# RWKV scan: larger VectorE products, copies on ScalarE, a norm's scratch in another buffer, and a 32-column operand

## The chip, the cores and the metric

One Trainium2 chip, one core. The metric is the device time of one execution in microseconds: the median of several runs. A core has TensorE (PE, matmuls), VectorE (DVE), ScalarE (ACT), GpSimd (POOL), SyncE (SP, here the queue of the DMAs), a memory SBUF of 128 partitions, and PSUM banks into which TensorE writes.

## What is computed

The reference is a network of two layers over 1024 latent tokens and 256 context tokens of width 1024. Each layer normalises, modulates with vectors made from the conditioning input (`ada_w`, `ada_b`), projects, mixes tokens with four groups side by side (mLSTM, Hyena, retention, RWKV-7), projects back, and runs a convolutional feed-forward block. What the change touches:

```
mod  = split(silu_c @ ada_w[l] + ada_b[l], 6)
u    = modulate(layer_norm(x), mod[0], mod[1])
...
sa    = einsum('bhvk,bhk->bhv', s_mem, at)
s_new = s_mem*wt[:,:,None,:] + sa[...,None]*bt[:,:,None,:] + vt[...,None]*kt[:,:,None,:]
y     = einsum('bhvk,bhk->bhv', s_new, rt)
...
out = g * (head_group_norm(from_heads(h), ng, nb) + bonus)
```

The middle part is the RWKV-7 recurrence, run forward and backward over the tokens, first over the context and then over the latent tokens, 4 heads of width 64. All is in float32.

## The kernel before

**Stages.** A layer runs: modulation vectors and layer norms; the input projections, each as three matmuls over high and low halves of both operands (lines 1022 to 1024); the scan stage (RWKV scan, mLSTM and, as side work, the modulation vectors that come later); output projection; feed-forward. In the profiled execution layer 0's scan stage lies at about 760 to 1240 us, layer 1's at 2945 to 3390 us.

**The RWKV scan** works in ten steps of 128 tokens, forward and backward direction together (index `d`), and two chunks of 64 in each step. Per step:

- `rwkv_prep` (L472): decays, the operands `ar` (tile AR) and `bk` (tile BK), and their products `G` on TensorE. `bk` is multiplied by a part of `rkk` (L515) and by a decay (L526).
- `rwkv_inverse` (L546): the inverse of a unit triangular matrix. LM is a transposed copy of `NB` (L550, VectorE); 31 rounds of a product (L557) and a sum (L558) follow, each on what the one before left, most of it on GpSimd (62 instructions), a smaller part on VectorE. LM has one buffer.
- `rwkv_tail` (L562): transposes of the inverse into XT, two groups of small matmuls with Q between them, and four copies of corners into XT, in turn on ScalarE (L590) and VectorE (L591).
- `rwkv_chain` (L594): the recurrence, four times one after the other (two chunks, two directions). Each takes U (L614), a matmul, two copies into VSA (L617, the first on ScalarE, the second on VectorE), and an update of the state SV with the factor rho (L624). rho comes from four small products per step (L601), into one of two buffers.
- `group_norm` (L645) for two tiles of 128 tokens at a time, as soon as both directions of them are summed in YF: after steps 1 (layer 0 alone), 6, 7, 8 and 9. Its scratch is `gq`, which then goes out by DMA to `yw` (L659). Scratch and LM lie in the same pool under different names.

In the program's text a step s runs inverse(s+1), chain(s), group norm, tail(s+1), prep(s+2). **The order that runs is made by a scheduler**: it estimates times and puts each engine's instructions in one order, in which they then run; waits between engines are semaphores, and a buffer that is taken again waits for those who used it before. So a small edit can move instructions of other stages.

**Modulations.** `ada_steps` (L958) takes, per unit, 16 matmuls (L973) with the 128x128 weights as the loaded operand's partner and `k.sc[:,q]`, 2 columns (token and context), as the operand that is loaded; it leaves two rows of results at partitions 0 and 32 of a bank. `ada_out` (L937) copies them to `ab` (L940, two VectorE copies of 2x128), transposes (L941), and adds the bias (L944). `ada` (L948) does the same with larger blocks at the kernel's start.

**The layers' ends.** The output weights `wo` are loaded and split into halves in 32 pieces (`load_wo`, L1037: ScalarE L1015, VectorE L1016) into memory that the mLSTM's tiles hold until it has ended.

Of the kernel before, what the change touches and what calls it, by code (L numbers as in the profile page):

```python
# [429 lines left out]
def rwkv(K,l,pv,last,p1,p2,p3):  # L430
# [39 lines left out]
def rwkv_prep(K,C,s):  # L470
# [42 lines left out]
    for a in range(2):  # L513
        for ft in range(2): act(out=bk[:,:,ft,:,a],in_=As[:,:,ft].rearrange("p d (c t) -> p d c t",t=64),func=ACTF.Identity,scale=C['kas'][:,a,0,ft:ft+1],bias=C['kas'][:,a,1,ft:ft+1])
        for d in range(2): tt(out=bk[:,d,:,:,a],in0=bk[:,d,:,:,a],in1=v4(rkk[:,d,4-2*a:6-2*a]),op=A.mult)  # L515
    G=p.tile([128,2,2,2,2,128],F32,tag="G",name="G",bufs=3); bt=p.tile([128,2,2,2,2,64],F32,tag="BKT",name="bt",bufs=3)
    NB=p.tile([128,2,4,32],F32,tag="NB",name="NB")
    for d in range(2):
# [7 lines left out]
        for a in range(2): tt(out=bk[:,d,:,:,a],in0=bk[:,d,:,:,a],in1=Wi,op=A.mult)  # L526
# [34 lines left out]
def rwkv_tail(K,C,P):  # L561
# [26 lines left out]
    for q in range(2):  # L588
        lo=slice(q*64,q*64+32); hi=slice(q*64+32,q*64+64)
        act(out=XT[lo,0,:,hi],in_=bv[lo],func=ACTF.Copy)  # L590
        nc.vector.tensor_copy(out=XT[hi,1,:,lo],in_=bv[hi])  # L591


def rwkv_chain(K,C,P,Pn,s):  # L594
# [4 lines left out]
    for i in range(2):  # L599
        if i and not Pn: break  # L600
        for d in range(2): tt(out=rho[:,i,d],in0=io[:,1,d,:,i^d],in1=(Pn if i else P)['io'][:,0,d,:,d if i else 1-d],op=A.mult)  # L601
    need_y=not(C['last'] and s<2); YF=C['YF']
    if need_y: y=K.ybank(); yb=[y[:,0:256],y[:,256:512]]
    for i in range(2):
        for d in range(2):
# [11 lines left out]
            act(out=VSA[0:64,d,ch,0],in_=bv[0:64],func=ACTF.Copy); nc.vector.tensor_copy(out=VSA[64:128,d,ch,1],in_=bv[64:128])  # L617
# [310 lines left out]

def ada_bias(k,todo,pool):

    o=load_rows(k,[((l,g),rows(k.a['ada_b'][l:l+1,g*1024:g*1024+1024]),8) for l,g in todo],"adab",pool)
    for l,g in todo:
        if g in (1,4): k.nc.vector.tensor_scalar(out=o[l,g],in0=o[l,g],scalar1=1.0,scalar2=None,op0=ALU.add)
    return o


def ada_out(k,l,c0,n,ps,ab,t,bias):  # L937

    nc=k.nc; G=ab.shape[0]//32; e=n//128
    for j in range(G): nc.vector.tensor_copy(out=ab[32*j:32*j+2],in_=ps[32*j:32*j+2,0:n])  # L940
    for i in range(e): nc.tensor.transpose(t[:,i*G*32:(i+1)*G*32],ab[:,i*128:i*128+128],k.ident[0:G*32,0:G*32])  # L941
    m,j0=c0//1024,c0%1024//128
    tv=lambda v: v.rearrange("p (j i) s -> p j i s",i=e)
    nc.vector.tensor_tensor(out=tv(k.modc[:,m,j0:j0+G*e]),in0=t[:,0:e*G*32].rearrange("p (i j r) -> p j i r",i=e,r=32)[:,:,:,0:2],  # L944
        in1=tv(bias[l,m][:,j0:j0+G*e].unsqueeze(2).to_broadcast([128,G*e,2])),op=ALU.add)


def ada(k,l,g,pool,ab,loads,bufs,bias):  # L948

    nc=k.nc; b=k.dbank()  # L950
    for q in range(8):
# [451 lines left out]
def tile_backbone(ctx,tc,aps,out):  # L1403
# [42 lines left out]
```

## Time and profile before

| | us |
|---|---|
| median of 3 runs | 4264.0 |
| lowest, highest | 4252.06, 4266.33 |
| the profiled execution | 4269.9 |
| its span (first to last instruction) | 4268.0 |
| TensorE busy | 3956.8 (93%) |
| VectorE busy | 2672.2 (63%) |
| ScalarE busy | 1416.9 (33%) |
| GpSimd busy | 979.7 (23%) |

The shares are averages over stages of different kinds: the projections keep TensorE full, the scan stages don't. In a row of a profile, L550 is line 550, `LM<-NB` says which tile is written from which, and what stands after "idle before" or in square brackets is how long the engine stood idle just before and what ended that.

### The profile page before, as it was taken

Reading aid. Unit: us, or ns where it says so; the run is one execution under the profiler, and the core shown is the slowest. Engines: PE = TensorE matmul, PEld = TensorE weight load, DVE = VectorE, ACT = ScalarE, POOL = GpSimd, SP = SyncE. Lnnn points to the kernel's source line nnn. Section 1 sums busy time; section 2 is a strip of 40 time slices with the busy share of each in tenths; the row PEclk is TensorE's granted clock in tenths of the full one; section 3 lists DMA queues with packets and bytes.
Section 4 is the critical chain, followed back from the end, with each engine's and each line's share of the span. In section 5 each row is a group of like instructions: output and inputs, shape, how many; then the busy total and the mean of one; then the engine's idle time right before and its main releaser. Section 6 shows DMA issues by size and latency. Waiting matters only on the chain.

```text
span 4268.0 us, 65334 instructions
## 1 busy us (share of the span) xinstructions
PE 3956.8 (93%) x24976; PEld 3210.9 (75%) x24976; DVE 2672.2 (63%) x5412; ACT 1416.9 (33%) x2855; POOL 979.7 (23%) x2158
## 2 busy tenths in 40 slices
PE   5999999699979999999997999996899899999998
PEld 3878877566668888888884688885666678888886
DVE  5655665789769444444449555676888684444447
ACT  4433343554344211211123433344544342112121
POOL 3320023466512000000021221024666320000002
PEclk6999999789989999999998999997899699999999
DMA  4235444343343111111113235553332431111112
GB/s 166 74 102 177 149 153 122 112 143 116 122 160 119 45 40 34 41 40 35 37 35 124 82 91 154 169 162 114 122 115 84 136 114 55 48 41 55 45 50 99
DMA packets 477138, 414.16 MB, mean 97 GB/s; under 512 B 48827, under 2 KB 443284, under 8 KB 474010
## 3 DMA queue, kind: packets, MB, share of 16 engines
q1 hardware_dynamic: 476826, 409.99, 31.0%
q8 instruction: 197, 3.23, 0.3%
q14 instruction: 115, 0.94, 0.1%
HBM read 323.65 MB, written 86.25 MB: 96 GB/s over the span
## 4 chain that ended last, share of the span: by engine, by line
PE 52%; DVE 11%; DMA 3%; issue 2%; POOL 1%; ACT 1%; SPq 0%; ACTq 0%; DVEq 0%; POOLq 0%
PE bank L1022 9%; PE bank L1023 9%; PE bank L1024 9%; PE dbank L1022 6%; PE dbank L1023 6%; PE dbank L1024 6%; DVE bst L983 1%; DMA xt<-x 1%; DVE facc L1205 1%; PE bank L186 1%; PE bank L187 1%; DMA wst<-in_w_out 1%; PE dbank L529 0%; DVE facc L1206 0%; DVE facc L1274 0%
## 5 line engine op out<-in xcount | busy, mean ns | idle before, releaser
L1022 PE MATMUL dbank<-uh,wh 128*128 128x512 f32 (+1 forms) x2120 | 765.3, 370 | 8.8 <-ACT tmpB L398 5.7
L1023 PE MATMUL dbank<-ul,wh 128*128 128x512 f32 (+1 forms) x2120 | 761.2, 368 | 0.0
L1016 DVE TENSOR_TENSOR wl<-wst,wh 128x1024 fp32r<-128x1024 f32 x146 | 185.5, 1272 | 491.9 <-ACT wh L1015 367.3
L1024 PE MATMUL dbank<-uh,wl 128*128 128x512 f32 (+1 forms) x2120 | 480.6, 367 | 0.0
L1022 PEld LDWEIGHTS dbank<-uh,wh 128*128 128x128 f32 x2120 | 401.4, 189 | 85.0 <-ACT tmpB L398 6.1
L1023 PEld LDWEIGHTS dbank<-ul,wh 128*128 128x128 f32 x2120 | 401.6, 189 | 68.9 <-issue 1.1
L1024 PEld LDWEIGHTS dbank<-uh,wl 128*128 128x128 f32 x2120 | 365.9, 188 | 70.5 <-issue 1.5
L1264 DVE TENSOR_TENSOR facc<-facc,bank 128x512 f32<-128x512 f32 x324 | 221.8, 686 | 205.1 <-PE bank L1024 205.1
L1022 PE MATMUL bank<-uh,wh 128*128 128x512 f32 (+1 forms) x920 | 334.9, 372 | 4.5 <-ACT uh L1010 4.5
L1233 POOL MEMSET fz<- 128x1 f32 x132 | 7.2, 98 | 1433.6 <-DVE fc L1248 1433.6
L1023 PE MATMUL bank<-ul,wh 128*128 128x512 f32 (+1 forms) x920 | 335.1, 372 | 0.8 <-DVE ul L1011 0.8
L1022 PE MATMUL bank<-wdh,gh 128*128 128x512 f32 x792 | 314.9, 400 | 17.9 <-DVE facc L1278 8.7
L1023 PE MATMUL bank<-wdl,gh 128*128 128x512 f32 x792 | 310.5, 392 | 1.0 <-DVE wdl L1016 1.0
L1024 PE MATMUL bank<-wdh,gl 128*128 128x512 f32 x792 | 248.1, 392 | 0.0
L1015 ACT ACTIVATE wh<-wst 128x1024 fp32r<-128x1024 f32 x146 | 154.8, 1060 | 238.1 <-PE dbank L1023 168.4
L1015 ACT ACTIVATE wdh<-wst 128x1024 fp32r<-128x1024 f32 x46 | 48.8, 1062 | 529.4 <-PE bank L1024 427.7
L558 POOL TENSOR_TENSOR XL<-XL,lt 128x48 f32<-128x48 f32 (+26 forms) x620 | 204.4, 330 | 47.7
L557 POOL TENSOR_TENSOR lt<-LM,XL 128x48 f32<-128x48 f32 (+26 forms) x620 | 187.1, 302 | 119.4 <-ACT XL L551 45.0
L1024 PE MATMUL bank<-uh,wl 128*128 128x512 f32 (+1 forms) x920 | 211.9, 372 | 0.0
L1022 PEld LDWEIGHTS bank<-uh,wh 128*128 128x128 f32 x920 | 174.1, 190 | 36.1 <-ACT uh L1010 5.6
L1023 PEld LDWEIGHTS bank<-ul,wh 128*128 128x128 f32 x920 | 174.2, 189 | 31.9 <-DVE ul L1011 1.7
L1022 PEld LDWEIGHTS bank<-wdh,gh 128*128 128x128 f32 x792 | 149.7, 189 | 59.4 <-DVE facc L1278 14.9
(476 smaller groups left out, 8132.3 us busy)
## 6 DMA issues: line engine op xcount, KB each, us to landing
wst<-in_ffn_w_up SPq DMA_DIRECT2D x88, 512.0 KB
adaw<-in_ada_w SPq DMA_DIRECT2D x160, 256.0 KB
wst<-in_w_in SPq DMA_DIRECT2D x58, 512.0 KB
wst<-in_ffn_w_down SPq DMA_DIRECT2D x46, 512.0 KB
df<-in_c_F SPq DMA_DIRECT2D x10, 1344.0 KB
xt<-x SPq DMA_DIRECT2D x26, 512.0 KB
df<-in_c_I SPq DMA_DIRECT2D x8, 1344.0 KB
rkk<-wrk SPq DMA_DIRECT2D x10, 1024.0 KB
```

The costliest lines, as they stand in the source:

```text
L186: mm(dst_re,F[:,i],pre(slot),start=True,stop=False); mm(dst_re,F[:,i+1],pim(slot),start=False,stop=True)
L187: mm(dst_im,F[:,i],qim(slot),start=True,stop=False); mm(dst_im,F[:,i+2],qre(slot),start=False,stop=True)
L557: e.tensor_tensor(out=t_,in0=LM[:,j,j+1:32].unsqueeze(2).to_broadcast([128,n,m]),in1=X[h][:,j:j+1,0:m].to_broadcast([128,n,m]),op=A.mult)
L558: e.tensor_tensor(out=X[h][:,j+1:32,0:m],in0=X[h][:,j+1:32,0:m],in1=t_,op=A.add)
L983: for h in range(2): nc.vector.bn_stats(out=st[:,h],in_=x[h])
L1015: k.nc.scalar.activation(out=h,in_=st,func=ACTF.Copy)
L1016: k.nc.vector.tensor_tensor(out=lo,in0=st,in1=h,op=ALU.subtract)
L1022: mm(ps,lh,rh,start=(i==0),stop=False)
L1023: mm(ps,lh,rl,start=False,stop=False)
L1024: for i,((lh,ll),(rh,rl)) in enumerate(pairs): mm(ps,ll,rh,start=False,stop=(i==n-1 and more is None))
L1205: for o,i,gg in zip([y[:,h] for h in hs],x,[g[:,h] for h in hs]) if parts else [(y,x,g)]: stt(out=o,in0=i,scalar=m,in1=gg,op0=ALU.subtract ...
L1264: else: tt(out=d,in0=d,in1=ps,op=ALU.add)
```

## The change

1. The two products of `bk` per direction become one over both directions (L515), and the two per operand become one over both operands (L526): 80 instructions of 128x256 become 40 of 128x512, on both lines.
2. The second VSA copy (L617, 80 instructions) and the second XT corner copy (L591, 40) go from VectorE to ScalarE. The rho products (L601, 76) go from VectorE to GpSimd.
3. The modulations' loaded operand has 32 columns, of which 30 are zero (`ada_sc`), so that all rows of the bank are written; one ScalarE copy of 64x128 (or 128x256) takes the place of 2 (or 4) VectorE copies of 2 rows.
4. The scratch `gq` of the RWKV scan's group norm no longer has its own buffer, but takes its turn in LM's.

```
-            group_norm(K,YF[:,sl],K.D['yw']...,2,p2.tile([128,8,64],F32,tag="gq",name="gq"),"gnw")
+            group_norm(K,YF[:,sl],K.D['yw']...,2,p2.tile([128,16,64],F32,tag="LM",name="gq"),"gnw")
...
-        for d in range(2): tt(out=bk[:,d,:,:,a],in0=bk[:,d,:,:,a],in1=v4(rkk[:,d,4-2*a:6-2*a]),op=A.mult)
+        tt(out=bk[:,:,:,:,a].rearrange("p d f c t -> p d (f c) t"),in0=bk[:,:,:,:,a].rearrange("p d f c t -> p d (f c) t"),in1=rkk[:,:,4-2*a:6-2*a].rearrange("p d f (c t) -> p d (f c) t",t=64),op=A.mult)
...
-        for a in range(2): tt(out=bk[:,d,:,:,a],in0=bk[:,d,:,:,a],in1=Wi,op=A.mult)
+        bka=bk[:,d].rearrange("p f c a t -> p (f c) a t"); tt(out=bka,in0=bka,in1=Wi.rearrange("p f c t -> p (f c) t").unsqueeze(2).to_broadcast([128,4,2,64]),op=A.mult)
...
-        nc.vector.tensor_copy(out=XT[hi,1,:,lo],in_=bv[hi])
+        act(out=XT[hi,1,:,lo],in_=bv[hi],func=ACTF.Copy)
...
-        for d in range(2): tt(out=rho[:,i,d],in0=io[:,1,d,:,i^d],...,op=A.mult)
+        for d in range(2): nc.gpsimd.tensor_tensor(out=rho[:,i,d],in0=io[:,1,d,:,i^d],...,op=A.mult)
...
-            act(out=VSA[0:64,d,ch,0],in_=bv[0:64],func=ACTF.Copy); nc.vector.tensor_copy(out=VSA[64:128,d,ch,1],in_=bv[64:128])
+            act(out=VSA[0:64,d,ch,0],in_=bv[0:64],func=ACTF.Copy); act(out=VSA[64:128,d,ch,1],in_=bv[64:128],func=ACTF.Copy)
...
+def ada_sc(k,pool):
+    s=pool.tile([128,8,32],F32,name="scz"); k.nc.gpsimd.memset(s,0.0); k.nc.gpsimd.tensor_copy(out=s[:,:,0:2],in_=k.sc)
+    return s
...
-    for j in range(G): nc.vector.tensor_copy(out=ab[32*j:32*j+2],in_=ps[32*j:32*j+2,0:n])
+    nc.scalar.activation(out=ab,in_=ps[0:G*32,0:n],func=ACTF.Copy)
...
-                for j in range(2): nc.tensor.matmul(ps[32*j:32*j+2,0:128],k.sc[:,q],w[u][q//2][:,q%2,j*128:j*128+128],start=(q==0),stop=(q==7))
+                for j in range(2): nc.tensor.matmul(ps[32*j:32*j+32,0:128],sc[:,q],w[u][q//2][:,q%2,j*128:j*128+128],start=(q==0),stop=(q==7))
```

**What it moves.** The scheduler makes a new order of the whole program. Three places, all in layer 0's scan; the rows are each engine's instructions in the order in which it runs them (line, operation, output from inputs, partitions x elements; numbers behind a name are buffer numbers, and `DMAHW2`, `Pool`, `Activation`, `PE` in brackets are those whose semaphores it waits for).

GpSimd at the group norm after step 7, before: it stands in the middle of inverse 9.

```order
L558 TENSOR_TENSOR XL<-XL,lt 128x48
L557 TENSOR_TENSOR lt<-LM,XL 128x44
L658 TENSOR_TENSOR gq<-YF,gn_r 128x512
L558 TENSOR_TENSOR XL<-XL,lt 128x44
L557 TENSOR_TENSOR lt<-LM,XL 128x40
```

GpSimd at the same norm, after the change.

```order
L557 TENSOR_TENSOR lt<-LM,XL 128x4
L558 TENSOR_TENSOR XL<-XL,lt 128x4
L658 TENSOR_TENSOR gq<-YF,gn_r 128x512
L758 TENSOR_TENSOR mRU<-mVO,cmbd 8x512 x2
L557 TENSOR_TENSOR lt<-LM,XL 128x31
L558 TENSOR_TENSOR XL<-XL,lt 128x31
```

The norm's product now stands between the last instructions of inverse 8 (128x4) and the first of inverse 9 (128x31). It is the same after steps 1 and 6.

VectorE at LM of inverse 8, before.

```order
L624 TENSOR_TENSOR SV<-cbank,rho 64x128 [waits PE_49]
L624 TENSOR_TENSOR SV<-cbank,rho 64x128
L515 TENSOR_TENSOR bk<-bk,rkk 128x4x64 [waits DMAHW2_49,Activation_49]
L515 TENSOR_TENSOR bk<-bk,rkk 128x4x64 [waits DMAHW3_49]
L550 STREAM_TRANSPOSE LM<-NB 128x1024 [waits Pool_49]
L565 STREAM_TRANSPOSE T_11516<-XL 128x128 [waits Pool_49]
```

VectorE at the same LM, after the change.

```order
L655 TENSOR_REDUCE gn_r<-gq 128x8 [waits Activation_49]
L657 RECIPROCAL gn_r<-gn_r 128x8 [waits Activation_49]
L530 TENSOR_TENSOR G<-dbank,rmask 128x512 [waits PE_49]
L785 TENSOR_TENSOR NUM<-NUM,mbank 128x260 [waits DVE_49,PE_49]
L624 TENSOR_TENSOR SV<-cbank,rho 64x128 [waits PE_49]
L624 TENSOR_TENSOR SV<-cbank,rho 64x128
L550 STREAM_TRANSPOSE LM<-NB 128x1024 [waits DMAHW2_49,Pool_49]
L624 TENSOR_TENSOR SV<-cbank,rho 64x128 [waits PE_49]
```

LM now stands behind the norm of step 6 (L655, L657) and behind the first state updates of chain 7, and waits for a DMA, the norm's output, beside GpSimd.

ScalarE at the end of the stage, before: the splits of the output weights come after everything of the scan and of the mLSTM.

```order
L1149 ACTIVATE yT<-dbank,pvm_1661 128x256 x4
L654 ACTIVATE gq<-mV 128x512
L656 ACTIVATE gn_r<-gn_r,eps_74 128x8
L1015 ACTIVATE wo_9225<-wst 128x256 x4
L1015 ACTIVATE wo_9227<-wst 128x256 x4
```

ScalarE at the end of the stage, after the change (lines from 929 on are 6 higher there: 1021 is 1015).

```order
L617 ACTIVATE VSA<-cbank 64x128 x2
L1021 ACTIVATE wo_9187<-wst 128x256 x4
L1021 ACTIVATE wo_9189<-wst 128x256 x4
L614 ACTIVATE U<-cbank 128x128
L1021 ACTIVATE wo_9191<-wst 128x256 x3
L617 ACTIVATE VSA<-cbank 64x128 x2
L1021 ACTIVATE wo_9191<-wst 128x256
L1021 ACTIVATE wo_9193<-wst 128x256 x4
```

Eleven splits now stand in front of the last pair of VSA copies of chain 9, and the mLSTM's last norm stands before them.

At the kernel's start the Hyena filter's first part (L273 matmuls and the GpSimd products of L139) moves from between the layer norms' instructions to behind them. The projections and the feed-forward keep their order but for a few places.

## Rows read from the trace of the kernel before

**Rows 1.** Page, part 2: busy tenths in 40 equal slices of the span.

```profile
PE   5999999699979999999997999996899899999998
...
DVE  5655665789769444444449555676888684444447
```

**Rows 2.** Window, layer 0's scan: length; busy (count) of PE, PEld, DVE, ACT, POOL; clock, DMA.

```profile
760.00:1240.00 480.00, 398.44 (x4616) 298.69 (x4615) 391.24 (x1168) 224.00 (x599) 254.67 (x696) 0.86 0.41 126
```

**Rows 3.** Lines 550, 617 by layer: ns min/median/max, first and last start.

```profile
L550 DVE STREAM_TRANSPOSE LM<-NB x10: 1924/1952/1967, 804.5 to 1121.8; 128x1024 f32<-128x1024 f32 x10
...
L617 DVE COPY VSA<-cbank x40: 286/295/296, 857.4 to 1196.1; 64x128 f32<-64x128 f32 x40
...
L550 DVE STREAM_TRANSPOSE LM<-NB x10: 1929/1958/1992, 2984.9 to 3322.0; 128x1024 f32<-128x1024 f32 x10
...
L617 DVE COPY VSA<-cbank x40: 290/295/296, 3038.5 to 3379.7; 64x128 f32<-64x128 f32 x40
```

**Rows 4.** Timeline, layer 0: start, duration us; steps 0 and 6.

```profile
839.12 1.96 DVE L550 STREAM_TRANSPOSE LM<-NB 128x1024 f32<-128x1024 f32 x1 [0.66 <-POOL lt L557]
...
872.51 0.29 DVE L617 COPY VSA<-cbank 64x128 f32<-64x128 f32 x1 [0.29 <-ACT VSA L617]
...
1085.42 1.97 DVE L550 STREAM_TRANSPOSE LM<-NB 128x1024 f32<-128x1024 f32 x1
...
1094.94 0.29 DVE L617 COPY VSA<-cbank 64x128 f32<-64x128 f32 x1
...
1115.68 1.05 POOL L658 TENSOR_TENSOR gq<-YF,gn_r 128x512 f32<-128x512 f32 x1
```

**Rows 5.** Timeline, layer 1: end of inverse 7 and the LM after it.

```profile
3267.10 0.37 POOL L558 TENSOR_TENSOR XL<-XL,lt 128x4 f32<-128x4 f32 x1
...
3286.21 1.93 DVE L550 STREAM_TRANSPOSE LM<-NB 128x1024 f32<-128x1024 f32 x1
```

**Rows 6.** Chain that ended last, both stage ends: start us, us, what.

```profile
1219.59 2.12 DMA ym<-gq
...
1238.99 0.77 PE bank L1022
...
3387.30 2.12 DMA yw<-gq
...
3390.64 0.80 PE bank L1022
```

**Rows 7.** Groups by form, VectorE, 770 to 1210: count, busy us, mean ns, idle.

```profile
L515 DVE TENSOR_TENSOR bk<-bk,rkk 128x256 f32<-128x256 f32 x40 | 17.8, 477 | 1.6 <-ACT bk L514 1.4
...
L940 DVE COPY ab<-mbank 2x128 f32<-2x128 f32 x48 | 13.4, 279 | 5.2 <-PE mbank L973 4.6
...
L617 DVE COPY VSA<-cbank 64x128 f32<-64x128 f32 x40 | 11.7, 294 | 5.1 <-ACT VSA L617 4.1
...
L791 DVE TENSOR_TENSOR NUM<-NUM,dn 128x512 f32<-128x512 f32 x9 | 6.4, 706 | 0.1
...
L591 DVE COPY XT<-cbank 32x128 f32<-32x128 f32 x20 | 5.8, 290 | 0.6
...
L601 DVE TENSOR_TENSOR rho<-io 128x2 f32<-128x2 f32 x38 | 4.6, 162 | 0.2
```

**Rows 8.** Timeline, layer 0, tail of step 5: first and last of four XT copies.

```profile
1026.30 0.25 ACT L590 ACTIVATE XT<-cbank 32x128 f32<-32x128 f32 x1
...
1030.47 0.30 DVE L591 COPY XT<-cbank 32x128 f32<-32x128 f32 x1
```

**Rows 9.** Groups by form, GpSimd, 770 to 1210: the smallest product.

```profile
L558 POOL TENSOR_TENSOR XL<-XL,lt 128x4 f32<-128x4 f32 x10 | 2.0, 202 | 0.8
```

**Rows 10.** Groups by form, TensorE's loads, 770 to 1210: 2 and 32 columns.

```profile
L973 PEld LDWEIGHTS mbank<-adaw,sc 128*2 128x2 f32 x768 | 30.2, 88 | 23.3 <-DMA adaw<-in_ada_w 10.2 <-issue 1.8
...
L585 PEld LDWEIGHTS cbank<-XT,Q 32*32 32x32 f32 x160 | 3.9, 115 | 3.5 <-issue 1.8 <-ACT Q L579 1.2 <-ACT Ep L506 0.3
```

**Rows 11.** Timeline, GpSimd, the start: filter products between two subtractions.

```profile
82.18 1.41 POOL L139 TENSOR_TENSOR hh<-hh,wn 128x256 f32<-128x256 f32 x2
```

More of the change, by code (lines that the diff above doesn't have):

```diff
@@ L464, in rwkv @@
             sl=slice(a,b+1,b-a)
-            group_norm(K,YF[:,sl],K.D['yw'].rearrange("(t p) c -> p t c",p=128)[:,sl],2,p2.tile([128,8,64],F32,tag="gq",name="gq"),"gnw")
+            group_norm(K,YF[:,sl],K.D['yw'].rearrange("(t p) c -> p t c",p=128)[:,sl],2,p2.tile([128,16,64],F32,tag="LM",name="gq"),"gnw")
         if s+1<NS: rwkv_tail(K,C,st[s+1])
@@ L600, in rwkv_chain @@
         if i and not Pn: break
-        for d in range(2): tt(out=rho[:,i,d],in0=io[:,1,d,:,i^d],in1=(Pn if i else P)['io'][:,0,d,:,d if i else 1-d],op=A.mult)
+        for d in range(2): nc.gpsimd.tensor_tensor(out=rho[:,i,d],in0=io[:,1,d,:,i^d],in1=(Pn if i else P)['io'][:,0,d,:,d if i else 1-d],op=A.mult)
     need_y=not(C['last'] and s<2); YF=C['YF']
@@ L945, in ada_out, with ada @@
         in1=tv(bias[l,m][:,j0:j0+G*e].unsqueeze(2).to_broadcast([128,G*e,2])),op=ALU.add)
-def ada(k,l,g,pool,ab,loads,bufs,bias):
+def ada(k,l,g,pool,ab,loads,bufs,bias,sc):
     nc=k.nc; b=k.dbank()
@@ L953, in ada @@
         loads.append(nc.sync.dma_start(w,k.a['ada_w'][l,q*128:q*128+128,g*1024:g*1024+1024]))
-        for i in range(4): nc.tensor.matmul(b[32*i:32*i+2,0:256],k.sc[:,q],w[:,i*256:i*256+256],start=(q==0),stop=(q==7))
+        for i in range(4): nc.tensor.matmul(b[32*i:32*i+32,0:256],sc[:,q],w[:,i*256:i*256+256],start=(q==0),stop=(q==7))
     ada_out(k,l,g*1024,256,b,ab,k.dbank(),bias)
@@ L960, in ada_steps @@
     nc=k.nc; units=[(l,g*1024+p*256) for l,g in todo for p in range(4)]; w={}
-    bias=ada_bias(k,todo,pool); ab=pool.tile([64,128],F32,name="ab"); nc.gpsimd.memset(ab,0.0)
+    bias=ada_bias(k,todo,pool); ab=pool.tile([64,128],F32,name="ab"); sc=ada_sc(k,pool)
     def load(u):
@@ L1414, in tile_backbone @@
         loads=[]
-        ab=pa.tile([128,256],F32,name="ab"); nc.gpsimd.memset(ab,0.0)
+        ab=pa.tile([128,256],F32,name="ab"); sc=ada_sc(k,pa)
         bias=ada_bias(k,[(0,0),(0,1)],pa)
-        for g in range(2): ada(k,0,g,pa,ab,loads,6,bias)
+        for g in range(2): ada(k,0,g,pa,ab,loads,6,bias,sc)
         mc=k.modc[:,0:2].rearrange("p m j s -> p s m j")
```

## The prediction

> **What bounds the kernel now.** I read the slices of the whole span first (106.7 us each). TensorE is at nine tenths nearly everywhere; in slices 7 to 11 and 27 to 31, counted from 0, it falls to 6 to 9, while VectorE, elsewhere mostly at 4 to 6, rises to 6 to 9 [rows 1]. Those are the scan stages of the two layers, and the change works there. In layer 0's window VectorE is busy 391 of 480 us, TensorE 398, GpSimd 255 [rows 2]; no engine is full, so the stage is set by chains of waits, and I looked for the loops.
>
> There are two. The **inverse loop**: LM is transposed on VectorE, GpSimd works 62 products in order, then the next LM. The ten LMs start from 804.5 to 1121.8 in layer 0 and from 2984.9 to 3322.0 in layer 1 [rows 3], so nine periods of 35.3 and 37.5 us. The **chain loop**: tail and chain of a step, four pairs of VSA copies one after the other, and the next tail's second half behind them. Its last copy ends at 1196.4 and at 3380.0 [rows 3]. Chain 0, with nothing queued before it, ends 33.7 us after inverse 0 (LM of inverse 1 starts as that ends, 839.1; last copy 872.8); chain 6 ends at 1095.2, 9.8 us after the LM of inverse 8 has already started [rows 4]. So the chain loop is as slow as the inverse loop and lags it late in the stage. In layer 1 the inverse loop is also held up by VectorE's order: inverse 7 ends at 3267.5, and the LM that follows it starts at 3286.2, behind products of other work, 18.7 us late [rows 5]. This is the largest of nine such handovers; together they lose about 40 us in layer 1 and 11 in layer 0, where most LMs start as the inverse ends.
>
> After the last chain copy layer 1 needs 10.7 us until its next projection (3390.6), since the output weights were split beside the scan. Layer 0 needs 42.6 us (1196.4 to 1239.0): the mLSTM ends last, its output leaves at 1219.6, and only then are the weights loaded and split [rows 6].
>
> **The change part by part.** The profiled execution took 4269.9 us, 5.9 over the median of 4264.0; I sum differences and take them from the median.
>
> *Copies and products off VectorE.* The L940 copies (13.4 us in layer 0), L617's (11.7), L591's (5.8) leave it; the small rho products (4.6) too. Two 128x256 products of L515 take 954 ns; one of 128x512 between SBUF tiles takes 706 by L791 [rows 7], so 0.25 us is saved twenty times, and the same for L526: 10 us. In all some 45 of 391 us. That is no gain by itself, as VectorE isn't full; it pays where VectorE's order makes the inverse late. Of the 11 and 40 us I take 10 and 30 (none, if the new order puts other work in front of LM; all, if every LM finds VectorE free): **-40**, from -51 to 0.
>
> *The copies in the chain.* A VSA pair now goes back to back on ScalarE instead of waiting for VectorE in turn, and so do the four XT copies at the tail's end, which took 4.5 us (1026.30 to 1030.77) for 1.1 us of copying [rows 8]. I take 0.7 us for each of four pairs and 2.5 for the XT copies, 5 us a step. The chain then ends about 29 us after its inverse, the next inverse 35 after it: the chain loop is no longer a limit, and its lag ends. From the last LM to the last copy it was 74.6 us in layer 0 and 58.0 in layer 1 [rows 3]; with no lag 66 and 55: **-11** (from -20 to 0).
>
> *Output weights in layer 0.* In the new order mLSTM runs up to a step earlier, and ScalarE does the splits among the last chain's copies, as layer 1 did already. I give layer 0 an end of 13 us, 2 over layer 1's, for the splits that the last copies queue behind: 42.6-13 = **-30** (0, if the mLSTM still ends last).
>
> *rho on GpSimd.* Four products each as long as GpSimd's smallest, 0.20 us and 0.08 between [rows 9], are 1.1 us a step. About half of the steps have them inside an inverse, the others at its head, where GpSimd waits for LM anyway: 6 us a layer. With two buffers, rho of step s waits for the last SV of chain s-2; that chain now ends before, so I add 2: **+16** in both layers (0 to 40).
>
> *Group norm through LM's buffer.* This is the price. LM, gq and the next LM now follow each other in one buffer, at step 1 (layer 0) and at steps 6 and 7 (both). LM(s+2) can start only when chain s has ended, its norm is done and its output has left. From the last VSA copy to the end of that DMA the busy case took 24 us (1095.2 to 1116.7 for step 6, and some 2.6 for the DMA), the quiet one 9.4 (3380.0 to 3389.4) [rows 4, 6]; I take 17. Chain s ends 6 us before inverse s+1, so LM is 11 us late. Before, it did not wait at all. At step 7 the 11 us of step 6 have already pushed the inverse back, and the norm then comes in time: one late LM counts at step 1 and one for 6 and 7 together. Layer 0 pays 23, layer 1 pays 12: **+35**. Lower end 0; upper end with chains as late as now 26+34 and 30, so 90.
>
> *Modulations.* 1280 passes load 32 columns, not 2, and take the time of the moving 128 columns as before; the load of 2 columns takes 88 ns beside other passes, one of 32 takes 115 [rows 10]. At 27 ns each that is 35 us if none were hidden; they are side work of the scan, and TensorE's time there is not the limit: 0. By the Trainium skill's page "TensorE: Matmul & The Clock Gate", section "LDWEIGHTS (loading the stationary operand)", a load's time goes by its columns, P/1.2 ns, which would be 25 ns more for each; the rows agree within a few ns.
>
> *The start.* The hyena filter's first part goes behind the layer norms. In 80-100 us GpSimd works filter products (1.41 us for two at 82.2) between the ul subtractions that TensorE's first gates wait for [rows 11]. Without them the projections start up to 10 us sooner; the filter's small matmuls, some 7 us, fall into time in which TensorE is full: **-4** (-12 to +8).
>
> Sum: -40-11-30+16+35-4 = **-34**, and 4264-34 = **4230 us**.
>
> A second rule of the skill speaks against the change: by "SBUF — State Buffer", section "SBUF: two separate sides", a VectorE product with two SBUF inputs and a GpSimd instruction exclude each other for their whole length. By it rho's 76 products would also hold VectorE, an estimate of 15 us of its time in both layers, and the merged products would hold GpSimd 0.25 us longer at a time; no row above separates this, and the sum leaves it out.
>
> **The rivals.** *The norm holds the inverse (slower).* If the chains end no earlier against the inverse than now, step 1 costs 26, steps 6 and 7 together 34 in layer 0 and 30 in layer 1; rho then waits too (+40 at most, 16 taken), and the VectorE relief is eaten by the wait: -30-4+16+90 = +72, 4336. It turns the sign as soon as the norm costs more than the 69 us that the rest gains, two thirds of the way from my 35 to 90. For it: LM stands right behind the norm's DMA in VectorE's order, and everything behind LM waits too. Against it: waiting empties the queues, and the norm then runs like the quiet case.
>
> *The relief doesn't arrive (no change).* mLSTM still ends last in layer 0, or LM is as late as before in layer 1: -34+30 = -4, 4260. For it: GpSimd stays in one order, and mRU's waits are in it.
>
> *VectorE was the limit.* Then waits for the norm are filled with queued products and cost nothing: -34-35, 4195. For it: VectorE's share of 82% with LMs late behind it; against it: layer 0's handovers lose only 11 us.
>
> *The loads of 32 columns are not hidden:* 4230+35 = 4265.
>
> **How the numbers follow.** Chances: forecast 0.47, with its own range 4212 to 4250; norm holds the inverse 0.18 (most of it between 4277 and 4300, half of the full price); relief doesn't arrive 0.20; VectorE was the limit 0.13; loads 0.02. 0.3%, about what a measurement of this kernel can tell from no change, is 13 us: faster (under 4251) is 0.47+0.13 = 0.60, same 0.20+0.02 = 0.22, slower 0.18. The range reaches over the first rival's half price and down to the VectorE case: 4188 to 4290.
>
> **What would show it.** LM's ten starts in layer 0 should come every 34 us but for one gap of about 46 after step 1 and one after step 6, with LM waiting for the norm's DMA; if the gaps are over 55, the first rival holds. Chains should end before the next inverse. Layer 0's projection should start 13 us after the last copy, layer 1's as before. If the inverse period itself falls below 32 us, VectorE was the limit. A stage of TensorE-full work that changes by more than 5 us would make the reading wrong.

## The result and the profile after

The changed kernel takes 4306.4 us (median of 4 runs, 4303.3 to 4309.1); the kernel before, beside it on the same chip, 4258.0 (4 runs, 4249.4 to 4266.3). The ratio is 1.0111, 95% interval 1.0097 to 1.0124: **slower by 48 us**, where 34 less was forecast, and 16 us above the range's upper end. The profiled execution of after took 4305.8 us, 35.9 more than that of before, so its rows show most of the loss. Lines from 929 on are 6 higher in after.

The page of after, part 2, the rows that answer to [rows 1], with the clock's under them (107.6 us a slice):

```profile
PE   5999998789979999999998799998799699999998
DVE  4663675577768644444448654776878584444446
PEclk6999998588989999999999899998799799999999
```

Slices 6 and 7, counted from 0, stand out: TensorE at 8 and 7, its clock at 8 and 5. They lie at 646 to 861 us, **ahead of the scan and at its very start**, in a part on which the prediction spent a few sentences. VectorE is a little emptier in the scan's slices, as meant. The scan itself, by the source rows of lines 550 and 617, both layers (ns min/median/max, first and last start in us), to be laid beside [rows 3]:

```profile
L550 DVE STREAM_TRANSPOSE LM<-NB x10: 1914/1948/1975, 843.7 to 1215.2; 128x1024 f32<-128x1024 f32 x10
...
L617 ACT ACTIVATE VSA<-cbank x80: 253/272/274, 896.2 to 1269.7; 64x128 f32<-64x128 f32 x80
...
L550 DVE STREAM_TRANSPOSE LM<-NB x10: 1921/1960/2036, 3029.8 to 3375.9; 128x1024 f32<-128x1024 f32 x10
...
L617 ACT ACTIVATE VSA<-cbank x80: 254/272/276, 3083.0 to 3419.1; 64x128 f32<-64x128 f32 x80
```

Layer 0's first LM comes at 843.7 us, 39.2 later than the 804.5 of [rows 3], which is more than the whole difference of the two profiled executions. From first LM to next projection layer 0's stage takes 443.2 us (to the projection at 1286.9, below), 8.7 more than before; layer 1's 399.6 (to 3429.4), 6.1 less. What lies between and behind is 6 shorter in sum. So there are two questions: what happens ahead of 843.7, and why the scan gains so little.

**Ahead of the scan.** Windows of 40 us of the kernel before, which were not shown: length; busy (count) of PE, PEld, DVE, ACT, POOL; clock, DMA share, GB/s.

```profile
600.00:640.00 40.00, 34.33 (x164) 26.84 (x163) 31.20 (x48) 17.54 (x27) 22.97 (x37) 0.91 0.59 183
640.00:680.00 40.00, 40.00 (x219) 33.71 (x218) 23.55 (x25) 18.08 (x28) 16.97 (x20) 1.00 0.61 156
680.00:720.00 40.00, 35.88 (x214) 30.33 (x213) 24.35 (x36) 10.21 (x21) 17.56 (x28) 0.93 0.38 114
720.00:760.00 40.00, 37.90 (x244) 31.82 (x246) 19.58 (x38) 14.29 (x29) 9.41 (x10) 0.86 0.22 70
```

The same windows of after, and the one behind them:

```profile
600.00:640.00 40.00, 39.67 (x198) 30.44 (x197) 31.64 (x56) 19.87 (x28) 0.33 (x6) 1.00 0.48 137
640.00:680.00 40.00, 39.21 (x205) 31.98 (x204) 15.31 (x20) 13.49 (x21) 2.80 (x12) 1.00 0.78 211
680.00:720.00 40.00, 28.86 (x144) 24.66 (x144) 37.48 (x62) 7.82 (x20) 35.05 (x46) 0.77 0.44 126
720.00:760.00 40.00, 29.86 (x149) 24.80 (x149) 16.37 (x26) 10.15 (x19) 23.28 (x30) 0.67 0.19 60
760.00:800.00 40.00, 40.00 (x170) 35.74 (x170) 11.28 (x26) 8.84 (x20) 2.09 (x2) 0.50 0.05 15
```

GpSimd is what tells it. Before, it works 39.9 us of the 80 from 600 to 680; after, 3.1, and then some 58 us from 680 to 760. Nearly all of the first and 49 of the 58 are the retention's work: its rotation (L812) and its state updates (L826, L827). In TensorE's order before, the first of the retention's 240 instructions stand between the last projections (9, 9, 10 and 10 of them, with 72 passes of projections behind each, then 202); in after all 240 stand behind the last projection. The projections end at 690.9 us, 15 sooner than before's 705.9, since nothing breaks them up. Then the retention's chain of VectorE, GpSimd and short matmuls runs with nothing to fill its waits: from the last projection to the first LM it is 152.8 us, where it was 98.6. In the window of 690 to 850 us by line (the counts are of passes, two to a matmul here), before:

```profile
L852 PE MATMUL bank<-rqkv,rS 128*128 128x64 f32 x80 | 17.4, 302 | 4.1 <-DVE rS L849 4.1
...
L853 PE MATMUL bank<-rSS,rT 128*128 128x64 f32 x80 | 16.7, 293 | 2.1 <-POOL rSS L827 2.1
```

and after (count | busy us, mean ns | idle us ahead of it, and what ended that):

```profile
L852 PE MATMUL bank<-rqkv,rS 128*128 128x64 f32 x80 | 25.4, 420 | 1.9 <-DVE rS L849 1.9
L853 PE MATMUL bank<-rSS,rT 128*128 128x64 f32 x80 | 25.2, 422 | 6.1 <-POOL rSS L827 6.1
...
L820 PE MATMUL bank<-rqkv,k 128*128 128x64 f32 x80 | 14.8, 363 | 10.5 <-DVE rqkv L814 6.9 <-issue 2.9 <-DVE k L818 0.7
```

The reader is to see two losses. TensorE waits: 10.5 us ahead of L820, most of it for the rotated keys, and 6.1 ahead of L853 for a state that GpSimd writes. And the same 160 passes of L852 and L853 take 50.6 us instead of 34.1, because the clock that was granted is lower: 0.77 and 0.67 in the two windows with the waits, then 0.50 from 760 to 800, where TensorE is busy throughout.

**In the scan: the price of the norm.** Timeline of after, layer 0, around steps 1 and 6, and layer 1, step 6 (start us, us, instruction, and in brackets the idle time ahead of it and what ended it). In each: the end of the inverse and the last VSA copies of the chain (in the order in which they come), the norm's product, the next LM.

```profile
941.09 0.20 POOL L558 TENSOR_TENSOR XL<-XL,lt 128x4 f32<-128x4 f32 x1
...
949.61 0.56 ACT L617 ACTIVATE VSA<-cbank 64x128 f32<-64x128 f32 x2 [1.17 <-PE cbank L615]
...
964.51 1.32 POOL L658 TENSOR_TENSOR gq<-YF,gn_r 128x512 f32<-128x512 f32 x1 [10.11 <-DVE gn_r L657]
...
968.32 1.95 DVE L550 STREAM_TRANSPOSE LM<-NB 128x1024 f32<-128x1024 f32 x1 [0.59 <-DMA yw<-gq]
...
1151.63 0.55 ACT L617 ACTIVATE VSA<-cbank 64x128 f32<-64x128 f32 x2
...
1153.41 0.53 POOL L558 TENSOR_TENSOR XL<-XL,lt 128x4 f32<-128x4 f32 x1
...
1172.82 1.04 POOL L658 TENSOR_TENSOR gq<-YF,gn_r 128x512 f32<-128x512 f32 x1 [2.58 <-PE mbank L762]
...
1176.43 1.95 DVE L550 STREAM_TRANSPOSE LM<-NB 128x1024 f32<-128x1024 f32 x1 [1.26 <-DMA yw<-gq]
...
3306.95 0.20 POOL L558 TENSOR_TENSOR XL<-XL,lt 128x4 f32<-128x4 f32 x1
...
3314.54 0.56 ACT L617 ACTIVATE VSA<-cbank 64x128 f32<-64x128 f32 x2
...
3335.06 1.04 POOL L658 TENSOR_TENSOR gq<-YF,gn_r 128x512 f32<-128x512 f32 x1 [0.22 <-DVE gn_r L657]
...
3338.35 1.96 DVE L550 STREAM_TRANSPOSE LM<-NB 128x1024 f32<-128x1024 f32 x1 [1.92 <-DMA yw<-gq]
```

LM starts 27.0, 22.5 and 31.2 us after the inverse ended, each time as the norm's DMA lands. After step 1 the chain ended 8.9 us *after* the next inverse, and chain end to LM took 18.2 us; after step 6 it ended 1.8 before it in layer 0 and 7.9 after it in layer 1. The mean from chain end to LM over steps 1, 6 and 7 of both layers was 23.5.

**The end of layer 0's stage.** The mLSTM's last output is issued on the DMA queue (SPq), and the chain that ended last goes on from the scan's own norm:

```profile
1258.69 0.41 SPq L659 DMA_DIRECT2D ym<-gq  x1
...
1283.55 2.14 DMA yw<-gq
...
1286.90 0.79 PE bank L1028
```

In [rows 6] the mLSTM's output (`ym`) and the weights behind it ended the stage; now the scan's (`yw`) does, 16.9 us after the last chain copy.

### The profile page after: what moved, and what is told of

It is laid out like the page before. It is cut to its first block, busy times and chain, and to the rows that moved or that the text cites. A ratio compares the mean times of both kernels' runs of the same rounds, so it can differ in the third digit from the quotient of the medians.

```text
span 4304.0 us, 65317 instructions
## 1 busy us (share of the span) xinstructions
PE 3977.3 (92%) x24976; PEld 3251.0 (76%) x24976; DVE 2574.4 (60%) x5048; ACT 1455.9 (34%) x3013; POOL 1016.2 (24%) x2237
## 4 chain that ended last, share of the span: by engine, by line
PE 53%; DVE 8%; POOL 3%; issue 2%; DMA 2%; ACT 2%; SPq 0%; ACTq 0%; DVEq 0%; POOLq 0%
PE bank L1029 9%; PE bank L1028 9%; PE bank L1030 9%; PE dbank L1028 6%; PE dbank L1029 6%; PE dbank L1030 6%; POOL XL L558 1%; POOL lt L557 1%; DVE bst L989 1%; DMA xt<-x 1%; DVE facc L1211 1%; PE bank L187 1%; PE bank L186 0%; DVE facc L1212 0%; DVE facc L1280 0%
## 5 line engine op out<-in xcount | busy, mean ns | idle before, releaser
L557 POOL TENSOR_TENSOR lt<-LM,XL 128x48 f32<-128x48 f32 (+26 forms) x620 | 195.9, 316 | 113.8 <-ACT XL L551 37.4
```

The lines of the kernel that those rows point to most:

```text
L557: e.tensor_tensor(out=t_,in0=LM[:,j,j+1:32].unsqueeze(2).to_broadcast([128,n,m]),in1=X[h][:,j:j+1,0:m].to_broadcast([128,n,m]),op=A.mult)
```

## The experiments

Each kernel was timed beside the kernel before, in four groups, each on one chip; before's medians there were 4258.0 (after), 4260.2 (e1 to e4), 4261.3 (e5 to e8) and 4259.8 (e9 to e11). In a table first; differences below are of these medians, and stages are those of the profiled executions.

| kernel | median us (runs) | ratio to before [95%] |
|---|---|---|
| after | 4306.4 (4) | 1.0111 [1.0097, 1.0124] |
| e1: change without its part 3 | 4263.5 (10) | 1.0005 [0.9988, 1.0022] |
| e2: e1, `gq` in its own buffer | 4253.1 (9) | 0.9980 [0.9969, 0.9990] |
| e3: e2, rho on VectorE | 4260.3 (10) | 0.9992 [0.9973, 1.0010] |
| e4: before + the start's modulations | 4311.3 (4) | 1.0120 [1.0086, 1.0153] |
| e5: before + an unread tile of 1 KB | 4302.6 (4) | 1.0092 [1.0075, 1.0110] |
| e6: change, operand as a window of 184 B | 4276.4 (7) | 1.0035 [1.0022, 1.0048] |
| e7: before + norm in LM's buffer | 4278.0 (5) | 1.0037 [1.0023, 1.0052] |
| e8, e11: window in the constant, own `gq` | 4246.7 (6), 4242.3 (5) | 0.9967 [0.9946, 0.9989], 0.9964 [0.9951, 0.9977] |
| e9: e8, norm in LM's buffer | 4270.5 (11) | 1.0026 [1.0013, 1.0039] |
| e10: change, start as before | 4275.3 (5) | 1.0038 [1.0025, 1.0050] |

In the expectations A says that the loss lies ahead of the scan and comes of the start's modulations (A2: by the memory of their operand), B that it is the norm's wait, C that the inverse loop was the limit all along. Later letters are explained where they stand.

**e1, e2, e3: which part loses.** e1 takes the 32 columns and their copies out of the change; e2 gives `gq` its buffer back too; e3 puts rho back on VectorE as well.

```
e1, against after
-            nc.tensor.matmul(...,sc[:,q],...)
+            nc.tensor.matmul(...,k.sc[:,q],...)
-    nc.scalar.activation(out=ab,in_=ps[0:G*32,0:n],func=ACTF.Copy)
+    for j in range(G): nc.vector.tensor_copy(out=ab[32*j:32*j+2],in_=ps[32*j:32*j+2,0:n])
e2, against e1
-  p2.tile([128,16,64],F32,tag="LM",name="gq")
+  p2.tile([128,8,64],F32,tag="gq",name="gq")
e3, against e2
-  nc.gpsimd.tensor_tensor(out=rho[:,i,d],...)
+  tt(out=rho[:,i,d],...)
```

> The whole change but the modulations' 32 columns and ScalarE copy. Theory A (the changed kernel's loss of 48 us lies ahead of the scan: the modulations at the start move the order, retention falls behind the last projections and layer 0's first LM starts 39 us late): the first LM is back at about 805 us and the time at 4262, 4250 to 4275. Theory B (the loss is the norm's wait in LM's buffer): the time stays at 4295 or more, whatever the first LM does. Under both, LM of inverses 3, 8 (and 8 in layer 1) is 20 to 30 us late.

> As e1, and gq in its own buffer again: products, copies and rho alone. Theory A: the norm's wait also goes, which in the changed kernel came to about 98 us over five LMs, not all of it in the end time: 4215, 4195 to 4235. Rival C (the inverse loop was the limit all along, and with VectorE relieved nothing is gained without the wait either): 4245 to 4262, and e2 is no more than 15 us under e1.

> As e2, and rho on VectorE again: merged products and ScalarE copies alone. My term for rho was 16 us in both layers: 4200, 10 to 16 under e2. Rival: rho on GpSimd costs nothing, as it fits where GpSimd waits; then e3 is within 5 us of e2. If rho was even a relief of VectorE, e3 is above e2.

Measured 4263.5, 4253.1 and 4260.3: e1 as A has it, e2 38 us above A's 4215 and e3 60 above the 4200 expected. Without its modulations the change is worth nothing; without the norm's move too it gains 7 us against before, 0.1 to 0.3%. Layer 0's first LM is back at 804.4, 804.6 and 803.8 us in the three traces: the 39 us ahead of the scan belong to part 3 of the change. rho on GpSimd costs nothing that shows (e2 is 7 us *under* e3, intervals that overlap). And of e2's inverses, by line 550 in layer 0,

```profile
L550 DVE STREAM_TRANSPOSE LM<-NB x10: 1920/1957/1992, 804.6 to 1122.7; 128x1024 f32<-128x1024 f32 x10
```

the ten LMs take 318.1 us, 317.3 in [rows 3]: with VectorE relieved and no wait for the norm the inverse loop of layer 0 goes no faster. There C holds. The stages did get shorter in the traces, by 13 and 17 us in e2 and by 7 and 20 in e3, but the stretch from layer 0's projection to layer 1's first LM got 9 and 17 us longer; the last section shows where.

**e4: the start's modulations alone.** The kernel before, with 32 columns and one ScalarE copy in the blocks at the kernel's start and nowhere else.

```
-  for i in range(4): nc.tensor.matmul(b[32*i:32*i+2,0:256],k.sc[:,q],...)
+  for i in range(4): nc.tensor.matmul(b[32*i:32*i+32,0:256],sc[:,q],...)
...
+  if n!=128: nc.scalar.activation(out=ab,in_=ps[0:G*32,0:n],func=ACTF.Copy)
```

> The kernel before with the 32 columns and the one ScalarE copy in the modulations at the start alone (the function ada, not the scan's side work). Theory A: this alone moves retention behind the last projections: first LM of layer 0 at 835 to 850 us, the rest as before: 4295, 4280 to 4305. Rival (it takes the whole change together, or the order does no harm): first LM within 5 us of 804.5 and 4258 within 13.

Measured 4311.3, 51 us over before and 6 over A's range, first LM at 845.4. Theory A stands: the start's modulations, whose own work lies at the kernel's start, move the first LM by 41 us.

**e5: is it their work, or their memory?** The kernel before, with one more tile in the start's pool, of the size of the 32-column operand. It is set to zero and never read; nothing else is changed.

```
+ scz=pa.tile([128,8,32],F32,name="scz"); nc.gpsimd.memset(scz,0.0)
```

> The kernel before with one more tile of 1 KB per partition in the memory pool of the start, cleared once and never read; no other line is changed. Theory A2: the modulations at the start move the order through the memory that their 32-column operand takes, not through their work; with the tile alone the filter's first part has to wait for memory, retention falls behind the last projections, and it costs what the start's modulations alone cost: first LM at 835 to 850 us, 4305, 4285 to 4320. Rival (the work of the 32-column passes and of the ScalarE copy is what moves it): first LM at 805 and 4260, within 13.

Measured 4302.6, 41 us over before. Windows of this kernel, and its line 550 in layer 0:

```profile
600.00:640.00 40.00, 37.49 (x211) 30.28 (x210) 30.70 (x67) 18.07 (x30) 0.33 (x6) 1.00 0.45 125
...
680.00:720.00 40.00, 29.87 (x146) 24.81 (x144) 35.94 (x58) 7.63 (x19) 31.98 (x47) 0.81 0.41 117
...
760.00:800.00 40.00, 40.00 (x168) 35.17 (x167) 10.99 (x26) 8.48 (x19) 2.08 (x2) 0.50 0.06 20
```

```profile
L550 DVE STREAM_TRANSPOSE LM<-NB x10: 1927/1942/1989, 846.1 to 1161.0; 128x1024 f32<-128x1024 f32 x10
```

The picture is after's, row by row: GpSimd nearly idle to 680, 32 us of work in the next 40, the clock at 0.50 from 760, the first LM at 846.1. No instruction of the change is in this kernel. So A2: **one unread tile of 1 KB per partition at the start is enough**. In the order of TensorE of this kernel the retention's 240 matmuls stand behind the projections, as in after. This run alone doesn't tell the tile's memory from the GpSimd instruction that sets it to zero; e6, the next, has such an instruction on a smaller tile, and there the retention stays between the projections. Which of the scheduler's decisions tips, and at what size between 184 bytes and 1 KB, is not shown.

**e6: the change without that memory at the start.** The operand of the start's blocks need not be eight blocks of 32 columns with zeros (the scan's keeps them here): the two columns of step q can be the first of a window of 32 in one tile of 46 columns, 184 bytes. The 30 other columns then hold the vectors of later steps and zeros, and fill rows of the bank that are never read.

```
-  s=pool.tile([128,8,32],F32,name="scz"); ... copy(out=s[:,:,0:2],in_=k.sc)
+  s=pool.tile([128,46],F32,name="scw"); ... copy(out=s[:,0:16],in_=k.sc)
-  ...sc[:,q]...
+  ...sc[:,2*q:2*q+32]...
```

> The whole change, but at the start the 32 columns are a window of a tile of 46 columns (184 bytes a partition, not 1 KB; the columns behind the first two then hold other numbers, whose results nobody reads). Theory A2: retention stays among the last projections, first LM at about 805, and 43 to 50 us of the change's loss are gone: 4262, 4248 to 4275. Rival: the loss stays, 4295 or more, with the first LM late or with the scan longer.

Measured 4276.4: 30 us of the 48 are gone, where 43 to 50 were expected, and the first LM is at 798.5 us. What is left is 0.2 to 0.5%; the profiled execution has layer 0's stage 15 us longer than before's and all else together as much shorter.

**e7: the norm's move alone.** The kernel before with the one line of the change that puts `gq` into LM's buffer.

```
-  p2.tile([128,8,64],F32,tag="gq",name="gq")
+  p2.tile([128,16,64],F32,tag="LM",name="gq")
```

> The kernel before with the norm's scratch in LM's buffer alone. With the faster chain this cost 10 us (all but the modulations, with it 4263.5, without it 4253.1). Theory D (the wait counts from the chain's end, and the chain is slower here): LM of inverses 3 and 8 is 25 to 35 us late, and it costs 20 to 40: 4290, 4275 to 4305. Rival E (in layer 0 the stage ends with the mLSTM, not with the scan, so that most of a late LM is not in the end time): 4268, 4258 to 4275, with the same late LMs.

Measured 4278.0, 17 us over before: a time in D's range, three above E's. LM of inverses 3 and 8 is 24 us late in layer 0, as D has it but for a microsecond; that the stage gets little longer by it is as E has it. The ten LMs of layer 0 lie from 808.0 to 1177.2, 52 us longer than in [rows 3], but layer 0's stage is only 3 us longer than in before: the last copy follows the last LM sooner (53 us, 74.6 before), and the projection the last copy (14.9, 42.6 before). Layer 1's is 3 longer too. The other 8 of the 14 us by which the profiled execution is longer lie outside of the stages and were not located.

**e8, e11: both mended.** The whole change, with the window of 46 columns in the constant tile of the conditioning vector itself and `gq` in a buffer of its own; to make room, two small tiles of layer-norm statistics have one buffer less each.

```
-  k.sc=k.p_c.tile([128,8,2],F32,name="sc")
+  k.scw=k.p_c.tile([128,46],F32,name="sc"); ... k.sc=k.scw[:,0:16].rearrange("p (k s) -> p k s",s=2)
...
-  ...sc[:,q]...
+  ...sc[:,2*q:2*q+32]...
...
-  tag="bst",bufs=3 ... tag="bmv",bufs=6
+  tag="bst",bufs=2 ... tag="bmv",bufs=5
```

> The whole change with the norm's scratch in its own buffer: the 32 columns are everywhere a window of one constant tile of 46 columns, and the 56 bytes that it needs come from two small tiles of the layer norm (one buffer less each). Theory: no moved retention and no wait of LM, so at least as fast as products, copies and rho alone (4253): 4250, 4235 to 4262. If the modulations' copies on ScalarE let the mLSTM of layer 0 end sooner, layer 0's projection starts before 1220 us and the time is 4235 to 4245. Rival: the modulations bring nothing, 4253 within 6.

> The kernel of e8 once more, beside the two others on one chip, since the distance to them is what is read. Expected 4247 (4240 to 4255), a ratio of 0.994 to 0.999 to the kernel before.

Measured 4246.7 and 4242.3: 0.3 to 0.4% faster than the kernel before, 60 and 64 us faster than the change as it was made. It is the fastest kernel here.

**e9: the norm's price in the mended kernel.** e8 with the one line of e7. It ran beside e11.

> The kernel of e8 (whole change, the 32 columns a window of the conditioning operand's own tile, so that the retention stays between the last projections) with one thing put back: the group norm's scratch takes its turn in LM's buffer again, as in the change. Theory E (the norm's wait for LM's buffer is paid in full in the whole change): 4246.7 plus the 29.6 us by which e6 lies over e8, some 4270 to 4280, with LM of steps 2, 7 and 8 in layer 0 late by 30 us or more together and layer 0's projection under 20 us behind the last chain copy. Rival G (the norm costs what it cost without the modulations, e1 over e2, 10 us; the rest of e6's distance from e8 comes of the start's copy of the operand and its order): 4255 to 4260.

Measured 4270.5, against e11's 4242.3: **28 us**, near E's 29.6 and not G's 10. The profiled execution of e9 was its shortest (4250.6 of 4250.6 to 4281.6), so its total tells little; its places do. Line 550 of e9, both layers:

```profile
L550 DVE STREAM_TRANSPOSE LM<-NB x10: 1924/1947/1967, 792.7 to 1148.9; 128x1024 f32<-128x1024 f32 x10
...
L550 DVE STREAM_TRANSPOSE LM<-NB x10: 1899/1934/1991, 2965.6 to 3322.2; 128x1024 f32<-128x1024 f32 x10
```

and of e11:

```profile
L550 DVE STREAM_TRANSPOSE LM<-NB x10: 1918/1948/1974, 794.8 to 1109.3; 128x1024 f32<-128x1024 f32 x10
...
L550 DVE STREAM_TRANSPOSE LM<-NB x10: 1904/1962/2006, 2977.7 to 3304.3; 128x1024 f32<-128x1024 f32 x10
```

The ten LMs take 41.7 us more in layer 0 (356.2 against 314.5) and 30.0 more in layer 1. In this pair layer 0 gives all of it back: stage 422.4 us against 426.0. Layer 1 keeps 19.3 (408.9 against 389.6). Why layer 0 can give it back shows in the chain that ended last of e11:

```profile
1201.31 2.12 DMA ym<-gq
...
1214.77 3.23 DMA wst<-in_w_out
...
1220.77 0.77 PE bank L1028
```

The last VSA copy is at 1179.0, but the mLSTM's output leaves at 1201.3 and the weights' loads follow: from the last copy to the projection it is 41.8 us, where e9 needs 14.5. The scan had some 27 us to spare; another 18 come from the last LM to the last copy, which takes 51.7 us in e9 and 69.8 in e11. So the wait for the norm is hidden up to there, and beyond it the scan ends the stage. Other pairs go beyond: layer 0's stage is 9 us longer in e1 than in e2, 20 in e6 than in e8, and 17 in after itself than in e11.

Part of the 28 us goes with the clock. e9's runs have a median granted clock of 0.943, e11's of 0.948, and within each kernel the runs at a lower clock are by and large the longer ones. At 0.944 a run of e9 took 4268.9 and one of e11 4248.6; at 0.948 one of e9 took 4250.6 and two of e11 4241.2 and 4242.3. That is 20 and 9 us. Whether the norm's waits bring the lower clock about is not shown.

**e10: the scan's modulations.** The change, but the blocks at the start as before. Against e1 it has 32 columns and ScalarE copies in the scan's side work, with the operand's 1 KB per partition in that work's memory, and nothing else.

```
-  nc.scalar.activation(out=ab,in_=ps[0:G*32,0:n],func=ACTF.Copy)
+  if n==128: nc.scalar.activation(out=ab,in_=ps[0:G*32,0:n],func=ACTF.Copy)
+  else:
+      for j in range(G): nc.vector.tensor_copy(out=ab[32*j:32*j+2],in_=ps[32*j:32*j+2,0:n])
...
-  nc.tensor.matmul(b[32*i:32*i+32,0:256],sc[:,q],...)
+  nc.tensor.matmul(b[32*i:32*i+2,0:256],k.sc[:,q],...)
```

> The whole change but for the kernel's start: the modulations there keep their two columns and their VectorE copies, so that the start's memory and order are as before; those of the scan stages have 32 columns and one ScalarE copy, and the norm lies in LM's buffer. Against e1 this adds the scan's modulations alone. Theory F (the modulations cost nothing, as predicted): 4263.5, within 5 us. Rival H (they cost what e6 lies over e1, by their loads or by the order that they make of the norm): some 4276. First LM of layer 0 at about 804 us by both; the lateness of LM behind the inverse, 40 us in layer 0 in e1, tells which: by H 70 or more, or longer inverses.

Measured 4275.3, 12 us over e1: by its time H, and with e6's 4276.4 it agrees with e6's start costing nothing more. The sign that was set came out between: LM of layer 0 is 65 us late (43 in e1), but the inverses are as much shorter, and the ten LMs take 358.0 us (359.2 in e1). Its profiled execution, the shortest of its five, is as long as e1's (4270.9 against 4272.1), so no row of the trace shows where the 12 us lie; e1's ten runs alone spread from 4250.8 to 4278.6, and at a clock of 0.941 one run of e1 took 4272.1 and two of e10 4273.8 and 4275.3. With `gq` in its own buffer and the operand as a window the modulations cost nothing: e8 and e11 lie 6 and 11 us *under* e2. Which of the two makes the difference was not separated. This stays open.

## Why the prediction was wrong, point by point

The medians divide the 48 us like this: the start costs 30 (after against e6) to 31 (against e10), the norm 28 to 30 (e9 against e11; e6 against e8, which differ in the scan's operand as well), and all the rest gains 15 to 18 (e8, e11 against before). The sum is 41 to 46. The norm's part depends on the kernel around it: 10 in e1 against e2, 17 in e7 against before. The forecast had -4, +35 and, for the rest, -65.

**The start (-4; +30).** This step failed. I read from the order that the filter goes behind the layer norms, priced that, and took it that "the projections start up to 10 us sooner". The projections ended 15 us sooner, and the scan's start was late by 39. The step looked at the first 100 us and not at where the order ends, and the description of the change has the same hole: "The projections and the feed-forward keep their order but for a few places" left out that the retention's matmuls had moved from between the last projections to behind them. "A stage of TensorE-full work that changes by more than 5 us would make the reading wrong": that is what came, in a place where work of two stages had been mixed. No rival held it.

**Copies and products off VectorE (-40).** The mechanism was right in layer 1, and the size was off. LM's lateness behind GpSimd's end of the inverse there, 41 us over nine handovers before, is 11 in e11: the 30 us came, at inverse 7 for instance (end and next LM, layer 1 of e11; 18.7 us late in [rows 5], 5.0 here):

```profile
3264.15 0.20 POOL L558 TENSOR_TENSOR XL<-XL,lt 128x4 f32<-128x4 f32 x1
...
3269.39 1.98 DVE L550 STREAM_TRANSPOSE LM<-NB 128x1024 f32<-128x1024 f32 x1
```

But the ten LMs take only 10.5 us less (326.6 against 337.1): nine inverses without their lateness take 315 us in e11 and took 296 before. What VectorE no longer delays, the inverses take longer by, two thirds of it. One reason would be that GpSimd works its other products, rho among them, in one order with the inverse, and that those that fell into its waits for LM cost nothing before. The traces bear it out in part only: inside the nine inverses GpSimd works 38.8 us on other things in e11 and 25.5 before, and 185.9 and 176.8 on the inverse itself, but e2 has nearly the same (37.4 and 183.0) and inverses of 302. So the reason stays open. The step counted lateness as if the loop's other half were fixed. In layer 0 10 us of 11 were taken (16 by the end of GpSimd's part, the measure of layer 1's 40); from first to last LM e2 and e3 show none, and e11 shows 2.8.

**The chain's copies (-11) and rho (+16).** The lag from last LM to last copy went from 74.6 to 69.8 us in layer 0 and from 58.0 to 53.0 in layer 1 (e11): 10 us, as forecast, but layer 0's half of it lies before the mLSTM's end, which ended that stage in e11. rho: a term of its own cannot be seen (e2, e3), though each product takes longer on GpSimd in after, 330 ns, against 162 in [rows 7]; layer 1's nine inverses take 302 us with it on GpSimd (e2) and 300 without (e3).

```profile
L601 POOL TENSOR_TENSOR rho<-io 128x2 f32<-128x2 f32 x38 | 11.6, 330 | 15.8 <-DVE SV L624 15.6
```

The rule of the Trainium skill's page "SBUF — State Buffer", section "SBUF: two separate sides", by which these would shut out VectorE's products, shows no price in the totals: e2 and e3 differ by 7 us the other way.

**Output weights in layer 0 (-30).** Failed, and after's trace alone hides it: 16.9 us from the last copy to the projection, near the 13 forecast. In e2, e3 and e11 it is 43.7, 46.6 and 41.8, as it was before (42.6). The mLSTM doesn't end a step earlier: its output leaves 406 us after the first LM in e11, 415 in before and in after. The distance is short in after because the scan ends late, its last copy 11 us behind the mLSTM's output. "0, if the mLSTM still ends last" was the bound, and the rival "the relief doesn't arrive" named it; it held.

**The norm through LM's buffer (+35).** The mechanism was right: LM waits for the norm's DMA at the steps named, one large wait for steps 6 and 7 together, and another 8 to 10 us at step 7, where none was taken. The total, 28, is near too, by luck: two errors cancel. A wait is 22 to 31 us and not 11, since chain end to LM takes 23.5 us in the mean and not 17, and chains end from 2 us before to 9 after the next inverse and not 6 before. And a late LM is not paid in full at layer 0's end, for the reason that undid the term before: without the wait the mLSTM ends there last. Layer 0, which was to pay 23, gains 4 in e9 against e11, and pays 9 (e1 against e2) and 17 (after against e11), while its LMs take 41 to 57 us longer. By the sign that the prediction set, LM gaps over 55 us, the first rival holds (they are 57 after step 1 and 65 after step 6); its price of 90 does not.

**Modulations (0).** The loads grew as forecast: a load of 32 columns takes 114 ns where that of 2 took 88 and 32 of another kind 115 [rows 10].

```profile
L979 PEld LDWEIGHTS mbank<-adaw,scz 128*32 128x32 f32 x768 | 38.5, 114 | 18.7 <-DMA adaw<-in_ada_w 11.2 <-issue 2.1 <-ACT S L763 0.6
```

The 26 ns for 30 columns agree with an estimate of 25 by the rule of P/1.2 ns for P columns in "TensorE: Matmul & The Clock Gate", section "LDWEIGHTS (loading the stationary operand)", of the Trainium skill. No price of them shows where `gq` has its own buffer (e11 under e2); the 12 us of e10 stay open. The merged products took 709 ns, where 706 was taken:

```profile
L515 DVE TENSOR_TENSOR bk<-bk,rkk 128x512 f32<-128x512 f32 x20 | 14.1, 709 | 2.1 <-ACT bk L514 1.5 <-issue 0.5
```

## What to carry to other kernels

Where a scheduler makes the order, compare the order of every engine over the whole program, and above all where two stages are mixed: a tile of 1 KB that nothing reads cost 41 us here, 600 us behind the place where it was allocated. A chain that ends a stage must be named before any relief beside it is counted: in layer 0 the mLSTM ended last, so the faster scan counted little there and the wait for the norm only as far as it pushed the scan's end past the mLSTM's; in layer 1 the scan itself ended last. A handover's lateness is not the loop's gain: here two thirds of what was taken from it came back as longer inverses.

## What was not expected of the hardware

TensorE at its lower clock while it was busy without a gap. From 680 to 760 us of after it was busy 28.9 and 29.9 us of each 40, with waits between, and the mean granted clock fell to 0.77 and 0.67; from 760 to 800 it was busy 40.0 of 40.0 with 170 short passes at 0.50, the level of 1.2 GHz. e5 shows the same (0.81 from 680, 0.50 from 760). So here the stretch with waits was followed by work at the lower level that had no waits at all: the mean of an L852 pass went from 302 to 420 ns, and TensorE is busy 17 us longer with these two lines.

The clock also differed where TensorE had the same retention passes to do. From layer 1's last projection to its first LM, 96.3 us before, ten of the traces take 95 to 99 us at a mean granted clock of 0.78 to 0.82; e2, e3 and e7 take 108 to 113 at 0.67 to 0.68. The row of e2, and under it that of e11:

```profile
2872.00:2980.00 108.00, 77.34 (x452) 65.06 (x450) 64.42 (x100) 43.97 (x94) 44.31 (x63) 0.68 0.37 107
2880.00:2977.00 97.00, 68.23 (x469) 55.62 (x467) 68.86 (x106) 46.83 (x101) 49.11 (x69) 0.81 0.41 118
```

In e2 the clock is at 0.50 from 2912 to 2956 us; in e11 the stretch that answers to it, 2920 to 2964, has a mean of 0.88, and TensorE is busy 9 us less in the row shown. So in single executions a difference of 10 us can go with the clock, and a small gain wants medians of several runs, read beside their clocks.
